# A seven-quarter form of the fifth product from the third row group on, and another order of work in the first two groups

## The chip, the cores and the metric

The kernel runs on one core of one Trainium2 chip. The metric is device microseconds (us) of that core for one execution; a kernel's time is the median of several. Every other time here comes from one profiled execution of the kernel before, in which the program's own span is 1494.3 us. Engines are named as in the profile: PE (matrix multiply), DVE (vector), ACT (scalar), POOL (GpSimd), SP (the engine from whose queue nearly all DMAs go out).

## The reference

```python
B, S, D = 8, 2048, 2048          # x: (8, 2048, 2048) float32, w: (2048, 2048) float32
cs = np.cumsum(x, axis=1)
diff = cs - concatenate([zeros, cs[:, :-1, :]], axis=1)
return np.matmul(diff, w).astype(np.float32)
```

The difference of a running sum with itself one step earlier is x again, so what is computed is one matrix product: x as 16384 x 2048, times w, 2048 x 2048.

## The kernel before

**Rows.** The 16384 rows are 128 row tiles of 128 rows. The first four (tiles 0 to 3) are multiplied plainly in bf16 while w arrives. The other 124 go in 31 groups of four: `group_plain(4)` is the first group, `group(8)`, `group(12)`, `group(16)` are the second, third and fourth, and so on to `group(124)`. In a group, g and h = g + 2 are the upper row blocks of two pairs and g + 1 and h + 1 the lower ones.

**The outer scheme.** Each pair of row tiles and the whole of w are cut into 2 x 2 blocks, and seven products with sums of blocks take the place of eight: A11·B11, A12·B21, S1·T1, S2·T2, S3·T3, S4·B22 and A22·T4. S1 to S4 are sums of quarters of x (f16, made on DVE by `total`, 128x1024 each), T1 to T4 differences of blocks of w (made on DVE by `less`, once, in the first group, 8 pieces each). One product for one pair is 16 matmuls of 128x128 by 128x512 (`steps`, L514), so a group of two pairs has 14 x 16 = 224.

**The inner scheme.** A product for the two pairs together (32 matmuls) can itself be cut once more into seven quarter products of four matmuls (`quarter`, L533): 28. It needs quarter sums of the block of w on the right: Q1, Q2, Q3, Q4, held by a class `Inner` (in_2 for B21, in_3 for B22, in_4 for T4, in_5 for T1). `first()` makes Q1 and Q2 (8 pieces of 128x512), `fourth()` makes Q4 (4 pieces), `third()` makes Q3 in the place of t12 (4 pieces). It also needs sums of quarters of the left side, made by `one()` and `two()` of `sums_in`, four small sums on DVE. From the second group on A12·B21, S4·B22 and A22·T4 have this form: 212 matmuls. Where `five` is true, which is from the fourth group on (`g > PLAIN + 8`), S1·T1 has it too: 208.

**Banks and results.** The eight banks of PSUM are the pairs X and Y and the single banks q, e, v, w (Z and V are pairs in the first group). A result block c (128x512 f32) is begun by `keep` (ACT, L541: copy out of PSUM with a scale) and added to by `add` (DVE, L544: one PSUM bank times a scale plus c); `put` stores it from SP's queue. There are seven such c buffers in a list `free`: `pair()` takes two from its front, `put` appends at its end. In the first group C11h lies in the tile `inner` instead, in pieces 16 to 19, which only later hold quarter sums, so it doesn't go into the list (`del free[-2:]`). One set of four pieces, `flow` (`passed`), holds Q4 for three of the `Inner`s in turn: what is not at hand lies in a DRAM buffer and is stored by `keep_flow(i)` and fetched by `bring_flow(i)`.

**Tiles of x.** Each tile is loaded in two halves (`load`, SP), weighed (`weigh`, ACT, L112: sum of magnitudes of each row), given a scale (`scale_of`: two small instructions on DVE, L129 and L131, and one on POOL, L132, for the unit u), narrowed to f16 (`narrow`, ACT, L143) and transposed by DMA in two halves (`turn`, SP, L156) into one of four places, where it overwrites the tile of the group before.

**Order.** The order on each engine is written out by hand. Every instruction goes through `after(engine, ...)`, which pins it behind the last one of that engine:

```python
    def after(engine, ask):
        if engine in last:
            with tc.issue_after(last[engine].ins):
                said = ask()
```

So an engine works strictly in the order of the calls in `group_plain` and `group`, and an instruction that waits holds up all that stand behind it on its engine.

Of the kernel before, what the change touches and what calls it, by code (L numbers as in the profile page):

```python
# [10 lines left out]
def kernel(  # L11
# [6 lines left out]
    nc = tc.nc  # L18
# [11 lines left out]
    f32 = mybir.dt.float32  # L30
    ADD = mybir.AluOpType.add
# [44 lines left out]
# [4 lines that stand above are left out]
        else:  # L80
            said = ask()
        last[engine] = said[-1] if isinstance(said, tuple) else said
        return said
# [37 lines left out]
    def scale_of(t):  # L121
        if t < END:
            m2 = sums_of.pop(t)
            m = small.tile([P, 1], f32, name="m1")
            s = scales[t] = small.tile([P, 1], f32, name="s")
            u = unit[t] = units.tile([P, 1], f32, name="u")
            after(
                "dve",
                lambda: nc.vector.tensor_scalar(m, m2[:, :1], m2[:, 1:], TINY, ADD, MAX),  # L129
            )  # L130
            after("dve", lambda: nc.vector.reciprocal(s, m))  # L131
            after("pool", lambda: nc.gpsimd.tensor_scalar(u, m, uw, None, MUL))  # L132
# [4 lines left out]
    def narrow(t, sides=range(2)):  # L137
        if t < END:
            s = scales[t]
            for i in sides:  # L140
                after(
                    "act",
                    lambda: nc.scalar.activation(  # L143
                        narrowed(t)[:, ds(i * NH, NH)], where[t][i], COPY, scale=s
                    ),
                )
# [316 lines left out]
    def pair():  # L463
        return [one_c() for _ in range(2)]
# [5 lines left out]
    class Inner:  # L470
# [14 lines left out]
                self.Q4 = [spare.pop() for _ in range(4)]  # L485
            less(self.Q4, self.t21, self.Q2)

        def third(self):
            less(self.t12, self.t22, self.t12)

    passed = [flow[:, k, :] for k in range(4)]

# [3 lines left out]
    def bring_flow(i):  # L496
        after("sp", lambda: nc.sync.dma_start(flow, spill[i - 1]))

    def less(dst, p, q):
        for k in range(len(dst)):  # L500
            after("dve", lambda: nc.vector.tensor_tensor(dst[k], p[k], q[k], SUB))  # L501

    def total(dst, p, q, op):
        after("dve", lambda: nc.vector.tensor_tensor(dst.all, p.all, q.all, op))  # L504
# [21 lines left out]
    def product(to, a, b, first):  # L526
        for some in steps(to, a, b, first, 4):
            some()
# [21 lines left out]
    def adds(c, p, u):  # L550
        for n in range(2):
            add(c[n], p[n], u)
# [7 lines left out]
    def puts(c, t, h):  # L560
        for n in range(2):
            put(c[n], t, 2 * h + n)
# [26 lines left out]
    def group_plain(g, X, Y, Z, V):  # L589
        h = g + 2  # L590
        ug, uh, vg = unit[g], unit[h], unit[g + 1]
        A11g, A12g = parts(g)
        A11h, A12h = parts(h)
        A21g, A22g = parts(g + 1)
        A21h, A22h = parts(h + 1)
        S1g, S1h = S1
        S2g, S2h, S3g, S3h, S4g, S4h = A11g, A11h, A21g, A21h, A12g, A12h
        load(g + 4, 0)
        load(g + 4, 1)
        product(X, A11g, B11, True)  # L600
        for k in range(3):
            block(B22, 1, 1, k, "act")
        C11g = pair()
        keeps(C11g, X, ug)
        for k in range(3, KH):
            block(B22, 1, 1, k, "act" if k < 6 else "dve")
        product(V, A12g, B21, True)
        product(Y, A11h, B11, True)
        adds(C11g, V, ug)
        puts(C11g, g, 0)  # L610
        total(S1g, A21g, A22g, ADD)
        total(S3g, A11g, A21g, SUB)
        total(S2g, S1g, A11g, SUB)
        less(T2[:4], B22[:4], T1[:4])
        product(Z, A12h, B21, True)
        weigh(h + 1)
        C11h = [inner[:, ds(j, 2), :].rearrange("p a n -> p (a n)").bitcast(f32) for j in (16, 18)]
        keeps(C11h, Y, uh)
        scale_of(h + 1)
        narrow(h + 1)  # L620
        turn(h + 1)
        load(h + 4, 0)
        less(T2[4:], B22[4:], T1[4:])
        vh = unit[h + 1]
        product(V, S1g, T1, True)
        C22 = pair()
        keeps(C22, V, vg)
        total(S4g, A12g, S2g, SUB)
        product(X, S2g, T2, False)
        C12g = pair()  # L630
        keeps(C12g, X, ug)
        less(T3, B22, B12)
        product(V, S4g, B22, False)
        weigh(g + 4)
        scale_of(g + 4)
        narrow(g + 4)
        load(h + 4, 1)
        turn(g + 4)
        load(g + 5, 0)
        load(g + 5, 1)  # L640
        product(X, S3g, T3, False)
        total(S1h, A21h, A22h, ADD)
        total(S3h, A11h, A21h, SUB)
        total(S2h, S1h, A11h, SUB)
        adds(C11h, Z, uh)
        puts(C11h, h, 0)
        del free[-2:]
        adds(C12g, V, ug)
        puts(C12g, g, 1)
        product(Y, S2h, T2, False)  # L650
        C12h = pair()
        keeps(C12h, Y, uh)
        adds(C22, X, vg)
        puts(C22, g + 1, 1)
        total(S4h, A12h, S2h, SUB)
        product(Z, S1h, T1, True)
        weigh(h + 4)
        less(T4, B21, T2)
        scale_of(h + 4)
        C22 = pair()  # L660
        keeps(C22, Z, vh)
        narrow(h + 4)
        weigh(g + 5)
        product(Y, S3h, T3, False)
        in_2.first()
        in_2.fourth()
        load(h + 5, 0)
        load(h + 5, 1)
        scale_of(g + 5)
        adds(C22, Y, vh)  # L670
        puts(C22, h + 1, 1)
        product(Z, S4h, B22, False)
        in_2.third()
        adds(C12h, Z, uh)
        puts(C12h, h, 1)
        narrow(g + 5)
        turn(h + 4)
        product(X, A22g, T4, False)
        C21 = pair()
        keeps(C21, X, vg)  # L680
        puts(C21, g + 1, 0)
        turn(g + 5)
        load(g + 8, 0)
        load(g + 8, 1)
        product(Y, A22h, T4, False)
        weigh(h + 5)
        less(in_3.Q1, in_3.t12, in_3.t11)
        scale_of(h + 5)
        narrow(h + 5)
        less(in_3.Q2, in_3.t22, in_3.Q1)  # L690
        turn(h + 5)
        C21 = pair()
        keeps(C21, Y, vh)
        puts(C21, h + 1, 0)


    def group(g, X, Y, q, e, v, w):
        h = g + 2
        five = g > PLAIN + 8
        A11g, A12g = parts(g)  # L700
        A11h, A12h = parts(h)
        A21g, A22g = parts(g + 1)
# [51 lines left out]
        a11, a12, a22, s1, s2, s3, s4 = A2  # L754
        Q = in_2
        quarter(q, a11, Q.t11, True)
        add(C11g[0], q, ug)
        quarter(e, s1, Q.Q1, True)
        add(C11h[1], e, uh)
        if g == PLAIN + 4:  # L760
            total(S1g, A21g, A22g, ADD)
            total(S3g, A11g, A21g, SUB)
            total(S2g, S1g, A11g, SUB)
        quarter(v, a12, Q.t21, True)
        add(C11g[0], v, ug)
# [3 lines left out]
        quarter(e, s4, Q.t22, False)  # L769
        add(C11g[1], e, ug)  # L770
        put(C11g[1], g, 1)
        if g > PLAIN + 4:
            total(S1h, A21h, A22h, ADD)
            total(S3h, A11h, A21h, SUB)
        scale_of(next_g)
        narrow(next_g)
        if g > PLAIN + 4:
            total(S2h, S1h, A11h, SUB)
        go(P6g, 2)
        quarter(q, s3, Q.Q3, False)  # L780
        add(C11h[1], q, uh)
        put(C11h[1], h, 1)
        if g == PLAIN + 4:
            total(S1h, A21h, A22h, ADD)
            total(S3h, A11h, A21h, SUB)
            total(S2h, S1h, A11h, SUB)
        weigh(next_h)
        load(next_k, 1)
        total(S4g, A12g, S2g, SUB)
        go(P6g, 2)  # L790
        C12g = pair()
        keeps(C12g, X, ug)
        turn(next_g, [0])
        quarter(q, a22, Q.Q4, False)
        add(C11h[0], q, uh)
# [5 lines left out]
        if five:  # L801
            one()
            two()
        scale_of(next_h)
        narrow(next_h)
        load(next_l, 1)
        one, two, A3 = sums_in(
            S4g, S4h, (S2h.half(0), S2h.half(1), S4h.half(0), passing[2])
        )
# [6 lines left out]
        if five:  # L816
# [17 lines left out]
            quarter(w, b11, R.t11, True)  # L834
            add(C12g[0], w, ug)
            quarter(v, b12, passed, False)
            bring_flow(1)
            add(C12g[0], v, ug)
            put(C12g[0], g, 2)
            turn(next_g, [1])  # L840
# [53 lines left out]
            put(C12h[1], h, 3)  # L894
            scale_of(next_l)
        else:
            if g == PLAIN + 4:
                in_3.third()
            one()
            two()  # L900
            weigh(next_k)
            seven(A3, in_3, C12g, C12h, P7g)
            turn(next_g, [1])
            turn(next_h, [0])
            scale_of(next_k)
            narrow(next_k)
            Q = in_4 if g == PLAIN + 4 else in_5
            Q.first()
            product((v, w), S1g, T1, True)
            C22g = pair()  # L910
            keeps(C22g, (v, w), vg)
            adds(C12g, (v, w), ug)
            puts(C12g, g, 1)
            load(next_l, 0)
            Q.fourth()
            keep_flow(2 if g == PLAIN + 4 else 1)
            product((q, e), S1h, T1, True)
            C22h = pair()
            keeps(C22h, (q, e), vh)
            adds(C12h, (q, e), uh)  # L920
            puts(C12h, h, 1)
            if g > PLAIN + 4:
                bring_flow(2)
            go(P7g, 2)
            one4()
            two4()
            turn(next_k, [0])
            adds(C22g, X, vg)
            puts(C22g, g + 1, 1)
            if g == PLAIN + 4:  # L930
                in_4.third()
            go(P7h, 4)
            adds(C22h, Y, vh)
            puts(C22h, h + 1, 1)
# [35 lines left out]
        if next_g < END:  # L970
            less(passed, in_2.t21, in_2.Q2)
        turn(next_l, [1])
        if g == PLAIN + 8:
            in_5.third()

    banks = [bank(i) for i in range(8)]
# [35 lines left out]
```

## Time and profile before

| | |
|---|---|
| median of the runs | 1492.88 us (1492.49 to 1496.3, 3 runs) |
| the profiled execution, its own time | 1496.11 us |
| its span | 1494.3 us |
| PE busy | 1473.4 us, 99% |
| DVE busy | 1283.9 us, 86% |
| ACT busy | 913.6 us, 61% |
| POOL busy | 69.4 us, 5% |
| DMA queue of SP | 379.41 MB, 92.6% of 16 engines |
| granted clock of PE | 0.999 |

How to read it: a line of a group of instructions has the line of the code, the engine, the operation, result and operands with their shapes, the count, and the mean length of one. A matmul is counted with 379 ns, but matmuls overlap, and in a full row one starts every 0.216 us. An idle time in square brackets stands in front of the instruction that it precedes, with what ended it. The groups begin at 76.05 (the first), 127.47, 177.44, 223.69 and 270.94 us.

### The profile page before, as it was taken

The numbers are of one execution on the slowest core, as the hardware profiler recorded it, in microseconds if no ns is written. First come the engines' busy times: TensorE is split into PE (matmuls) and PEld (weight loads), VectorE is DVE, ScalarE is ACT, GpSimd is POOL, SyncE is SP. The second block draws the span as 40 slices with busy tenths as digits, with TensorE's granted clock in tenths as the row PEclk, the third lists the DMA queues.
The fourth block names the chain that finished last, engine by engine and source line by source line (L and its number), as shares of the span: only waits on it lengthen the run. The fifth ranks groups of instructions, "written<-read, shape, count | busy, mean of one in ns | idle before, by whom it ended". The sixth has DMA issues, their size and how long they took to land.

```text
span 1494.3 us, 21105 instructions
## 1 busy us (share of the span) xinstructions
PE 1473.4 (99%) x6793; PEld 663.4 (44%) x6799; DVE 1283.9 (86%) x2419; ACT 913.6 (61%) x1301; POOL 69.4 (5%) x136
## 2 busy tenths in 40 slices
PE   8999999999999999999999999999999999999998
PEld 3444444444444444444444444444444444444443
DVE  7997878888888888888888888888888888888887
ACT  5876565655666656666656656556657556656542
POOL 0110000000000000000000000000000000000000
PEclk9999999999999999999999999999999999999999
DMA  9999979999999999999999998999899999899973
GB/s 362 352 233 254 244 224 255 263 271 249 259 258 241 260 276 250 255 251 251 265 269 242 266 248 255 261 272 248 257 239 261 268 257 262 252 238 265 273 204 130
DMA packets 386255, 382.59 MB, mean 256 GB/s; under 512 B 275744, under 2 KB 275744, under 8 KB 386016
## 3 DMA queue, kind: packets, MB, share of 16 engines
q1 hardware_dynamic: 385584, 379.41, 92.6%
q0 software_dynamic: 560, 1.84, 0.3%
q8 instruction: 53, 0.87, 0.2%
q14 instruction: 58, 0.48, 0.1%
HBM read 180.88 MB, written 135.27 MB: 212 GB/s over the span
## 4 chain that ended last, share of the span: by engine, by line
PE 88%; DMA 5%; DVE 3%; ACT 2%; issue 1%; SPq 1%; DVEq 0%; ACTq 0%
PE b L533 45%; PE b L514 41%; DVE c L544 2%; PE b L250 2%; DMA W<-in_w_dram 2%; DMA F<-in_x_dram 2%; DMA x<-F 1%; DVE W L501 1%; ACT waste L112 0%; DMA W<-in_x_dram 0%; DMA out_dram<-wb 0%; ACT F L143 0%; SPq L156 0%; DVE x L504 0%; ACT wb L234 0%
## 5 line engine op out<-in xcount | busy, mean ns | idle before, releaser
L544 DVE SCALAR_TENSOR_TENSOR c<-b,u,c 128x512 f32<-128x512 f32 x1046 | 743.2, 746 | 161.6 <-PE b L533 91.5
L514 PE MATMUL b<-W,x 128*128 128x512 f16 x3072 | 717.4, 379 | 4.3 <-ACT c L541 3.5
L541 ACT ACTIVATE c<-b,u 128x512 f32<-128x512 f32 x494 | 315.9, 681 | 334.5 <-PE b L533 164.0
L514 PEld LDWEIGHTS <-x 128*128 128x128 f16 x3072 | 300.3, 98 | 369.1 <-issue 6.3
L143 ACT ACTIVATE F<-F,s 128x1024 f16<-128x1024 f32 x246 | 282.2, 1147 | 111.2 <-DVE s L131 107.2
L533 PE MATMUL b<-W,inner 128*128 128x512 f16 x1392 | 338.3, 379 | 0.0
L112 ACT ACTIVATE waste<-F 128x1024 uint8<-128x1024 f32 x246 | 259.6, 1055 | 107.5 <-DMA F<-in_x_dram 103.7
L533 PEld LDWEIGHTS <-inner 128*128 128x128 f16 x1744 | 170.6, 98 | 207.1 <-issue 1.6
L533 PEld LDWEIGHTS <-x 128*128 128x128 f16 x1560 | 152.4, 98 | 192.3 <-issue 12.2
L533 PE MATMUL b<-W,x 128*128 128x512 f16 x968 | 234.3, 379 | 1.7 <-DVE c L544 0.3
L504 DVE TENSOR_TENSOR x<-x,x 128x1024 f16<-128x1024 f16 (+1 forms) x214 | 120.5, 574 | 6.2 <-PE b L514 1.1
L132 POOL TENSOR_SCALAR u<-m,uw 128x1 f32<-128x1 f32 x124 | 64.4, 525 | 1311.3 <-DVE m L129 1303.3
L533 PE MATMUL b<-flow,x 128*128 128x512 f16 x352 | 90.3, 379 | 0.7 <-DVE c L544 0.7
L504 DVE TENSOR_TENSOR inner<-x,x 128x1024 f16<-128x1024 f16 (+1 forms) x122 | 67.5, 553 | 1.2 <-DMA x<-F 1.1
L533 PE MATMUL b<-inner 128*128 128x512 f16 x240 | 61.6, 379 | 1.1 <-DVE c L544 1.1
L250 PE MATMUL b<-wb,xP 128*128 128x512 bf16 x234 | 57.0, 393 | 5.4 <-ACT wb L234 3.8
L533 PE MATMUL b<-inner,x 128*128 128x512 f16 x240 | 61.6, 379 | 0.0
L112 ACT ACTIVATION_READ_ACCUMULATOR waste<-F 128x1 f32 x246 | 46.6, 190 | 0.0
L504 DVE TENSOR_TENSOR x<-inner,x 128x1024 f16<-128x1024 f16 x62 | 42.4, 684 | 3.2
L504 DVE TENSOR_TENSOR inner<-inner 128x512 f16<-128x512 f16 x112 | 42.4, 420 | 1.0
L501 DVE TENSOR_TENSOR flow<-W,inner 128x512 f16<-128x512 f16 x120 | 42.6, 416 | 0.0
L234 ACT CAST wb<-W 128x1024 bf16<-128x1024 f32 x32 | 32.2, 1059 | 15.6 <-DMA W<-in_w_dram 12.3
(56 smaller groups left out, 420.0 us busy)
## 6 DMA issues: line engine op xcount, KB each, us to landing
out_dram<-c SPq DMA_DIRECT2D x494, 256.0 KB, 4.1
F<-in_x_dram SPq DMA_DIRECT2D x246, 512.0 KB, 5.2
flow<-spill SPq DMA_DIRECT2D x57, 512.0 KB, 4.8
W<-in_w_dram SPq DMA_DIRECT2D x32, 512.0 KB, 10.0
W<-in_x_dram SPq DMA_DIRECT2D x16, 256.0 KB, 7.2
x<-F SPq DMA_TRANSPOSE x246, 4.0
out_dram<-o POOLq DMA_DIRECT2D x5, 256.0 KB, 4.1
out_dram<-o SPq DMA_DIRECT2D x5, 256.0 KB, 3.6
```

Of the source, the lines that this page charges most:

```text
L112: lambda: nc.scalar.activation(waste, where[t][i], ABS, scale=1.0 / ROW, accum_out=sums_of[t][:, i : i + 1],),
L132: after("pool", lambda: nc.gpsimd.tensor_scalar(u, m, uw, None, MUL))
L143: lambda: nc.scalar.activation(narrowed(t)[:, ds(i * NH, NH)], where[t][i], COPY, scale=s),
L234: after("act", lambda: nc.scalar.copy(b, wt))
L250: lambda: nc.tensor.matmul(ps[r][n], xP[:, r, ko, :], wb[h, ko][:, ds(n * NB, NB)], start=(ko == 0), stop=(ko == KO - 1),),
L501: after("dve", lambda: nc.vector.tensor_tensor(dst[k], p[k], q[k], SUB))
L504: after("dve", lambda: nc.vector.tensor_tensor(dst.all, p.all, q.all, op))
L514: said = nc.tensor.matmul(to[n], a[k], b[k][:, n, :], start=(first and k == 0), stop=(k == KH - 1), skip_group_check=True,)
L533: said = nc.tensor.matmul(to, a[k], b[k], start=(first and k == 0), stop=(k == 3), skip_group_check=True)
L541: after("act", lambda: nc.scalar.activation(c, p, COPY, scale=u))
L544: after("dve", lambda: nc.vector.scalar_tensor_tensor(c, p, u, c, MUL, ADD))
```

## The change

It has three parts.

In `group_plain`, T2's pieces are made in four portions instead of two. The first C22 gets a place in `inner` (pieces 20 to 23) and leaves the list `free`. Its keep, and the keep of the last C21, go ahead of the narrowings that stood before them on ACT. T4 is made in two halves with a scale between them. The weighing of tile h + 5 moves ahead of the keep of the first C21. On SP the turns of h + 4 and g + 5 are taken apart and moved, and the loads of g + 8 go behind the turns of h + 5.

In `group(8)`, the sums S1g and S3g go in front of the first adds, and S1h, S3h, S2h in front of the third quarter; scale and narrowing of the next g go behind it, the weighing of the next h behind a keep, and its scale and narrowing, with a load, behind `one()` and `two()`. in_5.first is new there, in_4.third goes to POOL, in_4.fourth with its store is later, in_5.third is new at the end.

`five` is true from `group(12)` on, one group sooner; there in_5.fourth and a store of flow stand where later groups fetch it.

```diff
-        def third(self):
-            less(self.t12, self.t22, self.t12)
+        def third(self, engine="dve"):
+            less(self.t12, self.t22, self.t12, engine)
...
-    def less(dst, p, q):
+    def less(dst, p, q, engine="dve"):
+        on = {"dve": nc.vector, "pool": nc.gpsimd}[engine]
         for k in range(len(dst)):
-            after("dve", lambda: nc.vector.tensor_tensor(dst[k], p[k], q[k], SUB))
+            after(engine, lambda: on.tensor_tensor(dst[k], p[k], q[k], SUB))
...
         product(Y, A11h, B11, True)
+        less(T2[:1], B22[:1], T1[:1])
         adds(C11g, V, ug)
         puts(C11g, g, 0)
+        less(T2[1:2], B22[1:2], T1[1:2])
         total(S1g, A21g, A22g, ADD)
         total(S3g, A11g, A21g, SUB)
         total(S2g, S1g, A11g, SUB)
-        less(T2[:4], B22[:4], T1[:4])
+        less(T2[2:6], B22[2:6], T1[2:6])
...
         keeps(C11h, Y, uh)
         scale_of(h + 1)
+        less(T2[6:], B22[6:], T1[6:])
+        vh = unit[h + 1]
+        product(V, S1g, T1, True)
+        keeps(C22g, V, vg)
         narrow(h + 1)
         turn(h + 1)
         load(h + 4, 0)
-        less(T2[4:], B22[4:], T1[4:])
-        vh = unit[h + 1]
-        product(V, S1g, T1, True)
-        C22 = pair()
-        keeps(C22, V, vg)
...
-        adds(C22, X, vg)
-        puts(C22, g + 1, 1)
+        adds(C22g, X, vg)
+        puts(C22g, g + 1, 1)
+        del free[-2:]
...
-        less(T4, B21, T2)
+        less(T4[:4], B21[:4], T2[:4])
         scale_of(h + 4)
-        C22 = pair()
-        keeps(C22, Z, vh)
+        less(T4[4:], B21[4:], T2[4:])
+        C22h = pair()
+        keeps(C22h, Z, vh)
...
         load(h + 5, 1)
+        turn(h + 4, [0])
         scale_of(g + 5)
...
         narrow(g + 5)
-        turn(h + 4)
+        weigh(h + 5)
+        turn(h + 4, [1])
+        turn(g + 5, [0])
         product(X, A22g, T4, False)
         C21 = pair()
         keeps(C21, X, vg)
         puts(C21, g + 1, 0)
-        turn(g + 5)
-        load(g + 8, 0)
-        load(g + 8, 1)
+        turn(g + 5, [1])
         product(Y, A22h, T4, False)
-        weigh(h + 5)
         less(in_3.Q1, in_3.t12, in_3.t11)
         scale_of(h + 5)
+        C21 = pair()
+        keeps(C21, Y, vh)
         narrow(h + 5)
         less(in_3.Q2, in_3.t22, in_3.Q1)
         turn(h + 5)
-        C21 = pair()
-        keeps(C21, Y, vh)
+        load(g + 8, 0)
+        load(g + 8, 1)
         puts(C21, h + 1, 0)
...
-        five = g > PLAIN + 8
+        five = g > PLAIN + 4
...
         quarter(q, a11, Q.t11, True)
+        if g == PLAIN + 4:
+            total(S1g, A21g, A22g, ADD)
         add(C11g[0], q, ug)
+        if g == PLAIN + 4:
+            total(S3g, A11g, A21g, SUB)
         quarter(e, s1, Q.Q1, True)
         add(C11h[1], e, uh)
         if g == PLAIN + 4:
-            total(S1g, A21g, A22g, ADD)
-            total(S3g, A11g, A21g, SUB)
             total(S2g, S1g, A11g, SUB)
...
         put(C11g[1], g, 1)
+        total(S1h, A21h, A22h, ADD)
+        total(S3h, A11h, A21h, SUB)
+        if g == PLAIN + 4:
+            total(S2h, S1h, A11h, SUB)
         if g > PLAIN + 4:
-            total(S1h, A21h, A22h, ADD)
-            total(S3h, A11h, A21h, SUB)
-        scale_of(next_g)
-        narrow(next_g)
-        if g > PLAIN + 4:
+            scale_of(next_g)
+            narrow(next_g)
             total(S2h, S1h, A11h, SUB)
...
         put(C11h[1], h, 1)
         if g == PLAIN + 4:
-            total(S1h, A21h, A22h, ADD)
-            total(S3h, A11h, A21h, SUB)
-            total(S2h, S1h, A11h, SUB)
-        weigh(next_h)
+            scale_of(next_g)
+            narrow(next_g)
+        else:
+            weigh(next_h)
...
         keeps(C12g, X, ug)
+        if g == PLAIN + 4:
+            weigh(next_h)
...
-        scale_of(next_h)
-        narrow(next_h)
-        load(next_l, 1)
+        if g > PLAIN + 4:
+            scale_of(next_h)
+            narrow(next_h)
+            load(next_l, 1)
...
-            bring_flow(1)
+            if g == PLAIN + 8:
+                in_5.fourth()
+                keep_flow(1)
+            else:
+                bring_flow(1)
...
         else:
-            if g == PLAIN + 4:
-                in_3.third()
+            in_3.third()
             one()
             two()
+            scale_of(next_h)
+            narrow(next_h)
+            load(next_l, 1)
             weigh(next_k)
             seven(A3, in_3, C12g, C12h, P7g)
             turn(next_g, [1])
             turn(next_h, [0])
+            load(next_l, 0)
             scale_of(next_k)
             narrow(next_k)
-            Q = in_4 if g == PLAIN + 4 else in_5
-            Q.first()
+            in_5.first()
             product((v, w), S1g, T1, True)
...
-            load(next_l, 0)
-            Q.fourth()
-            keep_flow(2 if g == PLAIN + 4 else 1)
+            in_4.first()
+            in_4.third("pool")
             product((q, e), S1h, T1, True)
...
-            if g > PLAIN + 4:
-                bring_flow(2)
             go(P7g, 2)
             one4()
             two4()
             turn(next_k, [0])
             adds(C22g, X, vg)
             puts(C22g, g + 1, 1)
-            if g == PLAIN + 4:
-                in_4.third()
+            in_4.fourth()
+            keep_flow(2)
             go(P7h, 4)
...
-        if g == PLAIN + 8:
+        if g == PLAIN + 4:
             in_5.third()
```

More of the change, by code (lines that the diff above doesn't have):

```diff
@@ L613, in group_plain @@
         total(S2g, S1g, A11g, SUB)
-        less(T2[:4], B22[:4], T1[:4])
+        less(T2[2:6], B22[2:6], T1[2:6])
         product(Z, A12h, B21, True)
         weigh(h + 1)
-        C11h = [inner[:, ds(j, 2), :].rearrange("p a n -> p (a n)").bitcast(f32) for j in (16, 18)]
+        C11h, C22g = (
+            [
+                inner[:, ds(j, 2), :].rearrange("p a n -> p (a n)").bitcast(f32)
+                for j in (i, i + 2)
+            ]
+            for i in (16, 20)
+        )
         keeps(C11h, Y, uh)
         scale_of(h + 1)
+        less(T2[6:], B22[6:], T1[6:])
+        vh = unit[h + 1]
+        product(V, S1g, T1, True)
+        keeps(C22g, V, vg)
         narrow(h + 1)
@@ L668, in group_plain @@
         load(h + 5, 1)
+        turn(h + 4, [0])
         scale_of(g + 5)
-        adds(C22, Y, vh)
-        puts(C22, h + 1, 1)
+        adds(C22h, Y, vh)
+        puts(C22h, h + 1, 1)
         product(Z, S4h, B22, False)
```

## The prediction

> **What bounds the kernel now.** I read the page's shares first (PE busy 99% of a span of 1494.3 us, DVE 86%, ACT 61%, POOL 5%), then the timeline of PE, which shows where a group of four row tiles begins, then the busy time between those beginnings. Columns of the first view: stretch and its length in us, busy us of each engine (instructions), granted clock, DMA share, GB/s.
>
> ```profile
> core 0: us, PE busy (x) PEld busy (x) DVE busy (x) ACT busy (x) POOL busy (x), PEclk, DMA share, GB/s
> 76.05:127.47 51.42, 49.46 (x225) 21.91 (x224) 45.10 (x89) 39.01 (x54) 4.63 (x5) 1.00 0.84 240
> 127.47:177.44 49.97, 47.26 (x213) 20.55 (x212) 38.31 (x85) 31.07 (x46) 3.05 (x5) 1.00 0.96 240
> 177.44:223.69 46.25, 46.20 (x214) 20.69 (x213) 36.12 (x73) 27.77 (x42) 2.46 (x4) 1.00 0.86 238
> 223.69:270.94 47.25, 45.37 (x210) 20.34 (x208) 40.28 (x80) 27.57 (x41) 1.92 (x4) 1.00 1.00 265
> 270.94:316.04 45.10, 45.05 (x210) 20.34 (x208) 39.30 (x76) 28.23 (x41) 1.92 (x4) 1.00 0.96 259
> 316.04:1443.54 1127.50, 1126.33 (x5202) 508.58 (x5201) 982.70 (x1876) 693.85 (x1002) 47.94 (x100) 1.00 0.95 256
> ```
>
> The last row is 25 groups of 45.10. The code orders 224 matmuls in the first group, 212 in the second and third, 208 after. A steady row of 64 (76.05 to 89.86) gives 0.2158 each, so 208 take 44.89 and a steady group loses 0.21. PE at full clock is the bound. Without stalls the first four would take 48.34, 45.75, 45.75 and 44.89; they lose 3.08, 4.22, 0.50 and 2.36. Only these groups' code changes; from the fourth on it is the same. If the first three took 48.34, 46.25 (the third's old length) and 45.10, and the fourth 45.10, the gain would be 194.89 - 184.79 = 10.1, the most there is. The timeline of PE (start, length, what, count, idle before it and its releaser) says where it lies:
>
> ```profile
> 93.31 4.40 PE L514 MATMUL b<-W,x 128*128 128x512 f16 x16
> 98.15 0.38 PE L514 MATMUL b<-W,x 128*128 128x512 f16 x1 [0.44 <-ACT c L541]
> 117.33 13.76 PE L514 MATMUL b<-W,x 128*128 128x512 f16 x63 [1.18 <-ACT c L541]
> 131.48 0.38 PE L514 MATMUL b<-W,x 128*128 128x512 f16 x1 [0.40 <-ACT c L541]
> 140.18 1.90 PE L514 MATMUL b<-W,x 128*128 128x512 f16 x8 [0.40 <-DVE x L504]
> 145.84 3.63 PE L514 MATMUL b<-W,x 128*128 128x512 f16 x16 [0.31 <-DVE x L504]
> 150.33 0.38 PE L514 MATMUL b<-W,x 128*128 128x512 f16 x1 [0.86 <-ACT c L541]
> 234.45 1.02 PE L533 MATMUL b<-inner 128*128 128x512 f16 x4 [1.11 <-DVE c L544]
> 241.38 1.02 PE L533 MATMUL b<-flow,x 128*128 128x512 f16 x4 [0.73 <-DVE c L544]
> ```
>
> Idle time understates a stall, as a last matmul counts 0.38: I take starts less counts by 0.2158.
>
> **First group.** (a) 112.32 to 117.33 holds 17 matmuls (3.67): 1.34 lost, since a keep on ACT waited 3.55 for a C buffer's store. One pair now lives in inner, so two buffers more are free at that point: gain 1.34. (b) 93.31 to 98.73 holds 17: 1.75 lost, to the last halves of T2 (on DVE at 94.59 to 97.07, after 2.12 idle in wait for a scale) and to the keep of V behind a narrowing. Now six T2 pieces precede the scale, and the keep runs at 95.3 to 96.6, so S4g·B22 can begin near 96.8. What is late next is S2h. ACT runs from 94.06 two pairs of keeps (1.25 each), the narrowing (2.33), a pair of keeps, and the weighing of tile 8 (2.37), to 102.5; the scale on DVE waits for it, and S1h, S3h, S2h (0.7 each, before at 102.72) still end near 105.0. PE wants S2h at 96.8 + 32 x 0.2158 = 103.7 and got to it before at 105.4: gain 0.4. The two early T2 pieces (1.24) put S1g at 88.2 to 88.9, before PE's 89.86. The turn of tile 7 goes out 1.3 later and lands (3.2 median in this stretch) just before S1h wants it. Together +1.8: the second group begins at 125.7.
>
> **Second group, to its fifth product.** (c) 131.48 and the start after it lose 0.55 + 0.36 = 0.91, the keep of C21h behind a narrowing (128.53 to 130.86). Now it comes first, at 125.9 to 127.1, for a need at 129.1: +0.9. The weighing of tile 11 (2.4) moves ahead of the keep of C21: ACT 121.95 to 124.3, keep to 125.55, PE's need 125.7. That is just hidden; a load landing 1 late would cost 1. The loads of tile 12 move behind the turns of tile 11 on SP, each turn 1.3 of issue: they go out near 132.1 (133.29 before), its weighing ends near 140.7, and its scale has its turn on DVE only at 141.6. (d) S1g and S3g move into DVE's idle 2.40 before the first add: of 0.57 lost at 140.18, 0.2 stays if the second turn of tile 9 (out at 128.2, 5.0 median in this stretch) lands at 133.2: +0.4. (e) 145.84 loses 0.48 for S2h; the totals now come before the add that frees bank q, which ends near 141.55 for a need of 141.2: 0.45 back, so 0. (f) 150.33 and its next lose 1.04 + 0.36 behind the weighing of tile 14, now behind the keep: +1.4. The scale of tile 14 goes behind one() and two(), near 148, ahead of the first add, whose bank is done at 147.7. So S1g·T1 starts near 154.6, 159.11 before.
>
> **Second group's end.** DVE gets in_5.first, 8 pieces x 0.355 = 2.83, in front of the adds; in_4.third (1.42) leaves it, in_5.third (1.42) comes after the last quarter. Before, that stretch idled 0.31 + 0.67 + 1.08 on DVE. The adds behind run some 1.5 later against PE; the quarter s3 waits for its bank 0.5 instead of 0.21: -0.3. GpSimd's four subtractions have no row. From below, DVE's 0.355 each; from above, ACT's 0.68 for 512 columns and POOL's longest small instruction, 1.36: 2.04. I take POOL's shortest, 0.28, and DVE's one-column-a-cycle pass, 0.75: 1.03 each, 4.1 in all. They start when in_4.first ends (near 163 on this scale) and are wanted near 171.5: hidden up to 2.1 each. The next unit waits behind them on POOL and is wanted a group later. But the two engines meet:
>
> ```profile
> 114.53 0.83 POOL L132 TENSOR_SCALAR u<-m,uw 128x1 f32<-128x1 f32 x1 [11.04 <-DVE m L129]
> 114.55 1.41 DVE L501 TENSOR_TENSOR inner<-W 128x512 f16<-128x512 f16 x4
> 122.13 0.28 POOL L132 TENSOR_SCALAR u<-m,uw 128x1 f32<-128x1 f32 x1 [6.78 <-DVE m L129]
> 122.15 1.39 DVE L544 SCALAR_TENSOR_TENSOR c<-b,u,c 128x512 f32<-128x512 f32 x2
> ```
>
> The same POOL instruction takes 0.28 beside adds and 0.83 beside SBUF subtractions. So they hold each other up; that a long POOL instruction holds DVE, no row shows. From below 0, from above 4.1 less 0.6 of slack in front of the quarter into X[0]: 3.5. The first falls beside adds; three meet one4, two4 and in_4.fourth, half of each: 1.5 - 0.6, I take -1.0. [...]
>
> **Third and fourth group.** Four matmuls fewer (32 to 28), 0.86, and the other form's own waits, 0.29: +1.15. in_5.fourth (1.42) stands where a 512 KB load stood; DVE then adds in one row from 254.19 to 259.73 on the old fourth group's clock, and the quarter into bank e at 260.37 needs one that ended at 259.0: -0.2 (from 0 to -1.4). For the fourth group, the chain of waits shows why it loses 2.15 over 45.10:
>
> ```profile
> 222.34 7.70 DMA x<-F
> 230.06 0.44 DVE inner L504
> ```
>
> A turn goes out 1.35 before the group ends, lands 7.70 later, and DVE starts the sums 6.37 after the beginning, against 3.30 in the group after (274.24). A third group in the new form ends as the later ones do: +2.15. But the second now has its flow stored late, between the stores of C22, and I put its turn at 1.6 before its end: the same fault one group sooner, from 0 to -2.15, taken as -1.2, since no load waits there for a store (2.5 on SP before).
>
> **Sum:** 1.8 + 0.9 + 0.4 + 0 + 1.4 - 0.3 - 1.0 + 1.15 - 0.2 - 1.2 + 2.15 = 5.1, all against the profiled span: 1494.3 becomes 1489.2. That execution took 1496.11 outside, while the runs have a median of 1492.88 (1492.49 to 1496.3); the difference I carry over: 1487.8.
>
> **Rivals.**
> 1. No lock and the turns in time: 5.1 + 1.0 + 1.2 = 7.3, 1485.6; all stalls gone, 1482.8. For it: the third group began without a wait after a tail of the same length. Against: new DVE work in the second group. Chance 0.15.
> 2. The lock whole, 3.5 for 1.0: 1490.3. For it, POOL's own 0.83; against, the first subtraction has adds beside it. 0.15.
> 3. DMA takes the early gain back (share 0.96 in the second group): turns of tiles 9 and 12's loads late, so (d) and (f) fail, 1.8, and the fourth group's 2.15 comes whole in the third, 0.95 more: 1490.5. For it, weighings there waited 1.58, 1.30 and 2.08 for loads. 0.10.
> 4. Slower: the lateness is carried on. Each steady group waits 0.21 at its last quarter for an add; DMA is at 0.95. If the tails settle later, every one of 28 groups pays: it decides from 5.1 / 28 = 0.18 each, and at twice that, 0.36, the time is 1487.8 + 10.1 = 1497.9. Against: the old fourth group was 2.15 late and the next took 45.10 at once. 0.12.
>
> The forecast has 0.48, with its own range 1486 to 1490 (the lock and the turns at their ends, not together). A measurement tells 0.3%, 4.5 us, from no change: 1488.4 and 1497.4 bound it. Of the forecast some 0.35 lies below 1488.4; with rival 1, faster 0.50; rival 4 slower, 0.12; the rest 0.38. The range, 1483.5 to 1494, leaves out most of rival 4 and the end of rival 1.
>
> **What would show it.** (a), (b): no idle for a C buffer near 115 and S2h·T2 starting near 105.0. (c), (f): no PE idle released by ACT's L541. Second group near 48.6, third 46.5, fourth 45.1. POOL: four instructions near 1 us, DVE subtractions longer beside them. Wrong if a steady group is not 45.10, or if the last quarter of the second group waits for POOL.

## The result and the profile after

The changed kernel takes 1489.86 us (median of 6 runs, 1488.87 to 1490.62), the one before 1494.82 (6 runs, 1492.49 to 1497.16): ratio 0.9966, 95% interval 0.9954 to 0.9979, or 4.96 us less. The forecast was 5.1 us less, or 1487.8 us, reckoned from the 1492.88 that the kernel before had in 3 runs; in 6 runs its median is 1.94 higher. The profiled execution of the changed kernel has a span of 1488.0.

The busy time between the group starts of the changed kernel (length, busy us of PE, weight loads, DVE, ACT, POOL, then clock, DMA share, GB/s):

```profile
core 0: us, PE busy (x) PEld busy (x) DVE busy (x) ACT busy (x) POOL busy (x), PEclk, DMA share, GB/s
75.15:124.84 49.69, 48.60 (x225) 21.79 (x224) 46.37 (x95) 39.43 (x56) 5.99 (x6) 1.00 0.94 260
124.84:174.36 49.52, 46.57 (x213) 20.64 (x212) 41.85 (x84) 30.54 (x43) 7.25 (x8) 1.00 0.82 225
174.36:219.54 45.18, 45.13 (x210) 20.32 (x208) 41.59 (x84) 26.80 (x40) 1.92 (x4) 1.00 0.95 269
219.54:264.64 45.10, 45.05 (x209) 20.34 (x208) 39.40 (x76) 28.91 (x42) 1.92 (x4) 1.00 0.95 261
...
309.74:1437.24 1127.50, 1126.33 (x5201) 508.60 (x5200) 982.63 (x1876) 694.36 (x1002) 47.95 (x100) 1.00 0.95 256
```

The first four groups take 189.49 instead of 194.89: 5.40 less. Another 0.90 of the span's difference lies in front of them (start at 75.15 instead of 76.05), where no code changed; over all profiles below that start lies between 74.71 and 76.78. The steady groups take 45.10 as before (1127.50 for 25). The third and fourth already run at that pace; the second has gained only 0.45. PE's timeline has the waits that are left:

```profile
92.42 10.60 PE L515 MATMUL b<-W,x 128*128 128x512 f16 x48
104.11 3.63 PE L515 MATMUL b<-W,x 128*128 128x512 f16 x16 [1.09 <-DVE x L505]
...
111.03 20.88 PE L515 MATMUL b<-W,x 128*128 128x512 f16 x96
...
152.79 7.07 PE L515 MATMUL b<-W,inner 128*128 128x512 f16 x32
...
165.67 1.02 PE L534 MATMUL b<-W,x 128*128 128x512 f16 x4 [0.63 <-DVE c L545]
168.52 1.02 PE L534 MATMUL b<-W,x 128*128 128x512 f16 x4 [1.83 <-DVE c L545]
...
173.49 1.04 PE L534 MATMUL b<-W,x 128*128 128x512 f16 x4 [0.49 <-DVE c L545]
```

All idle times that ACT ended (98.15, 117.33, 131.48, 150.33 before) are gone, and 96 matmuls run through from the first group into the second. Left in the first group is the wait for S2h; new are three waits for DVE's adds in the last 9 us of the second. DVE and POOL in front of them:

```profile
158.36 3.34 DVE L502 TENSOR_TENSOR W<-W 128x512 f16<-128x512 f16 x4
158.92 5.09 POOL L502 TENSOR_TENSOR W<-W,W 128x512 f16<-128x512 f16 x4 [4.13 <-DVE W L502]
161.62 3.33 DVE L502 TENSOR_TENSOR W<-W,W 128x512 f16<-128x512 f16 x4
164.88 1.40 DVE L545 SCALAR_TENSOR_TENSOR c<-b,u,c 128x512 f32<-128x512 f32 x2
```

Four subtractions took DVE 1.41 elsewhere; beside GpSimd's in_4.third the eight of in_4.first take from 158.36 to 164.88. From S1g·T1 (152.79) to the end the second group needs 21.57, against 18.33 before: 3.24 lost. The start of S1g·T1 before, from which the 18.33 are counted to 177.44:

```profile
159.11 7.07 PE L514 MATMUL b<-W,inner 128*128 128x512 f16 x32
```

### The profile page after: what moved, and what is told of

It reads as the page before. It is cut to its first block, busy times and chain, and to the rows that moved or that the text cites. A ratio compares the mean times of both kernels' runs of the same rounds, so it can differ in the third digit from the quotient of the medians.

```text
span 1488.0 us, 21123 instructions
## 1 busy us (share of the span) xinstructions
PE 1470.6 (99%) x6789; PEld 663.2 (45%) x6795; DVE 1293.4 (87%) x2430; ACT 913.8 (61%) x1301; POOL 74.5 (5%) x140
## 4 chain that ended last, share of the span: by engine, by line
PE 91%; DMA 3%; DVE 3%; ACT 2%; issue 1%; SPq 0%; DVEq 0%; ACTq 0%
PE b L534 47%; PE b L515 43%; DVE c L545 2%; PE b L250 2%; DMA W<-in_w_dram 2%; DMA F<-in_x_dram 1%; DVE W L502 0%; DMA W<-in_x_dram 0%; DMA out_dram<-wb 0%; ACT F L143 0%; ACT waste L112 0%; ACT wb L234 0%; ACT W L361 0%; ACT o L270 0%; ACT c L542 0%
## 5 line engine op out<-in xcount | busy, mean ns | idle before, releaser
L534 PE MATMUL b<-W,inner 128*128 128x512 f16 x1416 | 344.1, 379 | 0.0
L237 DVE TENSOR_REDUCE wmax<-W 128x1 f32<-128x1024 f32 x32 | 38.9, 1219 | 3.4 <-DMA W<-in_w_dram 2.0
```

The source lines that it names most:

```text
L237: lambda: nc.vector.tensor_reduce(wmax[:, i : i + 1], wt, AX.X, MAX, apply_absolute_value=True),
L534: said = nc.tensor.matmul(to, a[k], b[k], start=(first and k == 0), stop=(k == 3), skip_group_check=True)
```

## The experiments

All lengths are group lengths from one profiled execution each, read as above; a start inside a merged row is counted on at 0.2158 a matmul. `first_new`, `bring_pool` and `bring_act` change the kernel before, the others the changed one.

| run | first | second | third | fourth | sum | sum without the first |
|---|---|---|---|---|---|---|
| before | 51.42 | 49.97 | 46.25 | 47.25 | 194.89 | 143.47 |
| after | 49.69 | 49.52 | 45.18 | 45.10 | 189.49 | 139.80 |
| third_dve | 48.48 | 47.02 | 45.67 | 45.10 | 186.27 | 137.79 |
| third_dve_timed | 48.34 | 47.02 | 45.82 | 45.10 | 186.28 | 137.94 |
| third_late | 48.80 | 47.02 | 46.02 | 45.10 | 186.94 | 138.14 |
| third_half | 49.95 | 48.28 | 45.10 | 45.10 | 188.43 | 138.48 |
| split | 49.53 | 48.37 | 45.29 | 45.10 | 188.29 | 138.76 |
| idle_pool | 48.34 | 52.86 | 45.10 | 45.10 | 191.40 | 143.06 |
| no_five | 48.34 | 46.29 | 46.25 | 47.26 | 188.14 | 139.80 |
| first_new | 48.91 | 47.30 | 46.24 | 47.23 | 189.68 | 140.77 |
| first_old | 51.03 | 54.50 | 45.19 | 45.10 | 195.82 | 144.79 |
| c22_pair | 49.91 | 51.14 | 45.10 | 45.10 | 191.25 | 141.34 |
| bring_pool | 51.64 | 50.25 | 51.73 | 46.16 | 199.78 | 148.14 |
| bring_act | 51.59 | 50.55 | 46.81 | 45.10 | 194.05 | 142.46 |

### Does GpSimd hold DVE up, and how much for one instruction?

**third_dve:** the four subtractions back on DVE, in the same place.

```diff
-            in_4.third("pool")
+            in_4.third()
```

> in_4.third goes back to DVE at the place where it now goes to GpSimd. After the change DVE's eight in_4.first subtractions beside GpSimd's four took 6.6 us (158.36 to 164.95) instead of 2.83, and the second group's end lost 3.24 over its old 18.33. Theory (the two engines lock each other out): DVE needs 2.83 + 1.42 = 4.25 there, 2.4 less, and the second group falls from 49.52 to about 47.2, the third stays at 45.2 or grows by up to 1 as its turn goes out earlier against DMA. Rival (it is the added DVE work in front of the adds that makes the end late): moving 1.42 more to DVE makes the second group 50.5 to 51.

The timeline of PE's S1g·T1 and of DVE:

```profile
151.26 7.07 PE L515 MATMUL b<-W,inner 128*128 128x512 f16 x32
...
156.84 1.42 DVE L502 TENSOR_TENSOR W<-W 128x512 f16<-128x512 f16 x4
158.17 2.77 DVE L502 TENSOR_TENSOR W<-W,W 128x512 f16<-128x512 f16 x8
160.86 1.40 DVE L545 SCALAR_TENSOR_TENSOR c<-b,u,c 128x512 f32<-128x512 f32 x2
```

Twelve subtractions from 156.84 to 160.86, 0.335 each. From S1g·T1 to the end the group takes 19.07, which loses 0.74 instead of 3.24. The second group falls to 47.02; the third grows by 0.5, where DVE waits 0.89 for a turned tile before S1h. More work on DVE and less time: the added work was not the cause.

**third_half:** two pieces each.

```diff
-            in_4.third("pool")
+            less(in_4.t12[:2], in_4.t22[:2], in_4.t12[:2], "pool")
+            less(in_4.t12[2:], in_4.t22[2:], in_4.t12[2:])
```

> Two of the four in_4.third pieces stay on GpSimd, two go to DVE. Theory (lock, one GpSimd instruction holds DVE for about its own length): DVE's time from the first piece of in_4.first to the first add behind is 2.83 + 0.71 + 2 x 0.96 = 5.5 us, between 6.6 and 4.25, and the second group is near 48.4. Rival (added DVE work): near 50. Rival (a start-up cost of GpSimd's first instruction of this kind): nearly all of the 3.8 stays, group at 49.5 or more.

DVE's stretch up to the first add is 5.27 for ten subtractions, 3.35 of its own at 0.335. What GpSimd adds is 1.92 for two instructions, and 6.52 - 8 x 0.335 = 3.84 for four: 0.96 for each, with no start-up. The second group is at 48.28.

**idle_pool:** GpSimd subtracts quarters of B21 into flow, which nobody needs; third on DVE.

```diff
+            if g == PLAIN + 4:
+                less(passed, in_2.t11, in_2.t21, "pool")
             in_5.first()
...
-            in_4.third("pool")
+            in_4.third()
```

> in_4.third is on DVE as in the first of these runs, and in the second group GpSimd makes four subtractions nobody needs: quarters of B21 into flow, tiles that DVE's in_5.first beside it (blocks of T1 into other places) neither reads nor writes. Theory (lock of the two engines, whatever the tiles): in_5.first takes 2.83 + 3 to 4 us, each DVE subtraction beside GpSimd near 0.8 instead of 0.355. Rival (the two were slow because both read t12 and t22 of T4): in_5.first stays at 2.83.

DVE and POOL:

```profile
152.53 2.37 DVE L502 TENSOR_TENSOR W<-W 128x512 f16<-128x512 f16 x4
153.30 5.20 POOL L502 TENSOR_TENSOR flow<-W,W 128x512 f16<-128x512 f16 x4
154.82 3.96 DVE L502 TENSOR_TENSOR W<-W,W 128x512 f16<-128x512 f16 x3
...
159.04 1.40 DVE L545 SCALAR_TENSOR_TENSOR c<-b,u,c 128x512 f32<-128x512 f32 x2
```

The eight of in_5.first go from 152.53 to 159.04: 6.51, 3.83 more than their own 2.68, with no tile in common with GpSimd's. So it is the engines that meet, not the tiles. Their rows alternate: in the changed kernel GpSimd's start at 158.92, 160.09, 161.38 and 162.68, and DVE's long subtractions behind them at 159.03, 160.33, 161.62 and 162.92, one every 1.30, which is 0.335 + 0.96. So a GpSimd instruction here costs DVE 0.96. The second group as a whole, 52.86, is longer than these 3.83 explain, for a reason told at the end.

**split:** Q1 of in_4 in front of the adds into C12h, Q2 behind them.

```diff
-            in_4.first()
+            less(in_4.Q1, in_4.t12, in_4.t11)
             in_4.third("pool")
...
             puts(C12h, h, 1)
+            less(in_4.Q2, in_4.t22, in_4.Q1)
```

> GpSimd keeps in_4.third, but DVE makes only Q1 of in_4 (four pieces) before the adds into C12h, and Q2 behind them, so GpSimd runs mostly beside adds, which read one operand from PSUM, and beside DVE's idle time. Theory (lock only against two SBUF operands): Q1 takes up to 1.42 + 2, the adds stay at 1.40 a pair, the end of the second group loses 1 to 1.5 instead of 3.24, group near 47.5. Rival (GpSimd slows every DVE instruction): adds longer than 1.40 a pair, group 49 or more.

```profile
158.04 3.34 DVE L502 TENSOR_TENSOR W<-W 128x512 f16<-128x512 f16 x4
161.30 1.40 DVE L545 SCALAR_TENSOR_TENSOR c<-b,u,c 128x512 f32<-128x512 f32 x2
162.62 2.17 DVE L502 TENSOR_TENSOR W<-W,W 128x512 f16<-128x512 f16 x4
```

GpSimd runs from 158.59 to 163.50, across all three rows. Subtractions on both sides are longer (Q1 starts 3.26 before the adds, 1.34 of its own; Q2 2.10), the adds, with one operand from PSUM, keep their 1.40. That is the theory; but only a quarter of GpSimd's work fell beside the adds, and the group came to 48.37, not 47.5.

### Where do the other gains come from?

**first_new:** the kernel before with the first group's function of the change, and nothing else of it: its edit is the part of the change that lies in `group_plain`.

> The kernel before with only the first group's function of the change. Theory: first group 49.7, second 49.97 - 0.9 = 49.0, third 46.25 and fourth 47.25 as before; sum 192.2, 2.7 under before. Rival (loads of tiles 12 and the others come later against PE and the second group gives it back): second group 50.5 or more, sum near 194.9.

The expectation is beaten: the second group gains 2.67, not 0.9, with its own code unchanged. 0.92 of it is the expected one, the keep of C21h that now stands in front of a narrowing. Of the rest, 1.39 is the stall at 150.33 and 0.32 a part of that at 156.38. For the stall at 150.33, SP's queue says why. Before:

```profile
134.37 5.92 SPq L156 DMA_TRANSPOSE x<-F  x2
141.48 1.75 SPq L100 DMA_DIRECT2D F<-in_x_dram  x3
```

and with the first group's new order:

```profile
127.37 4.24 SPq L156 DMA_TRANSPOSE x<-F  x3
135.11 2.43 SPq L100 DMA_DIRECT2D F<-in_x_dram  x3
...
143.14 4.49 PE L514 MATMUL b<-W,x 128*128 128x512 f16 x20 [0.31 <-DVE x L504]
```

Before, the two turns of tile 11 held SP for 5.92, and the loads of tiles 14 and 13 behind them went out 14.0 after the group's start (127.47). Now three turns go through in 4.24, and the loads go out 9.4 after it (125.69). The weighing of tile 14 doesn't wait for DMA any more (2.08 before), so the keep that stands behind it and cost PE 1.39 at 150.33 is in time: the 20 matmuls from 143.14 run through. This is read from the queue; no run changes SP's order alone. The waits before 140.18 and 145.84, (d) and (e) of the prediction, stay (0.57 and 0.47).

**first_old:** the reverse, the changed kernel with the old first group.

> The changed kernel with the first group's function as it was before: order of T2 and T4, C22 in the ring of C buffers, keeps behind narrowings, turns and loads in the old order. Theory (the first group's stalls were local and are gone for good): the first group is 51.4 again, the second 49.5 + 0.9 = 50.4 or a little more, the third 45.2, the fourth 45.1. Rival (the lateness is absorbed by slack later): second group 48 to 49.

The second group takes 54.50, 4.1 more than expected. DVE and PE:

```profile
142.02 0.69 DVE L505 TENSOR_TENSOR inner<-x,x 128x1024 f16<-128x1024 f16 x1 [2.27 <-DMA x<-F]
...
144.88 1.50 PE L534 MATMUL b<-flow,x 128*128 128x512 f16 x4 [2.25 <-DVE c L545]
```

S1h now stands ahead of the add that frees bank q. With the old first group, tile 11's turns land late, DVE waits 2.27 at S1h, and the add and PE wait behind it: PE loses 2.42 there. The other 1.7 is a slow stretch of PE right behind that wait (told at the end). The stall at 150.33 is gone here too, as the keep now stands in front of the weighing. So with the old first group, the 2.43 that the new order saves at (d), (e) and (f) is lost again at S1h.

**no_five:** the fifth product's form and its sums as before; the new order of the first group and of the second up to its fifth product stays.

```diff
-        five = g > PLAIN + 4
+        five = g > PLAIN + 8
...
-            in_5.first()
+            Q = in_4 if g == PLAIN + 4 else in_5
+            Q.first()
...
-            in_4.first()
-            in_4.third("pool")
+            load(next_l, 0)
+            Q.fourth()
+            keep_flow(2 if g == PLAIN + 4 else 1)
```

> The changed kernel with the fifth product as before: plain in the third group, in_4's sums in the second and in_5's in the third, all on DVE; the new order of the first group and of the second up to its fifth product stays. Theory (new order and earlier form are separate gains): second group 46.5 to 47, third 46.25, fourth 47.25. Rival (the new order of the second group brings nothing once the first is mended): second group 47.3, as with the first group's new function alone.

46.29, 46.25 and 47.26, as the theory has it. So the second group's order is worth another 47.30 - 46.29 = 1.01: (d) and (e). Without the first group, whose length varies (below), the sum is 139.80, the very sum of the whole change: the earlier form of the fifth product, as written, brings nothing. With the subtractions on DVE it brings 139.80 - 137.94 = 1.86 (third_dve_timed; 2.01 by third_dve, 1.66 by third_late below).

**c22_pair:** the first C22 from the ring of C buffers again.

```diff
-        C11h, C22g = (
...
-        )
+        C11h = [inner[:, ds(j, 2), :].rearrange("p a n -> p (a n)").bitcast(f32) for j in (16, 18)]
...
+        C22g = pair()
         keeps(C22g, V, vg)
...
-        del free[-2:]
```

> The changed kernel, but the first C22 is taken from the ring of C buffers again instead of inner. Theory: ACT's keep of the second C22 waits for a store of C12g again (3.55 before), PE loses up to 1.34 near 111 to 117, first group 49.7 + 1.0 to 1.3. Rival (the earlier order has made the store early enough): first group 49.7 as now.

The 17 matmuls from 112.27 end at 116.47: 4.20 for 3.67, so 0.53 lost and not 1.34. With 1.03 lost at S2h that makes the first group 49.91. ACT's keep still waits 2.75, but it starts earlier. The result lies between theory and rival: the order around it had taken most of the 1.34. Its second group is longer for another reason, told at the end.

**bring_pool:** the fetch of flow in the old third group from GpSimd's queue instead of SP's.

```diff
-                bring_flow(2)
+                after("pool", lambda: nc.gpsimd.dma_start(flow, spill[1]))
```

> The kernel before, but in its third group the fetch of flow that waits on SP for the store of flow goes out from GpSimd's queue, so that nothing waits behind it. Theory (the old fourth group loses 2.15 because the turn of tile 18 goes out late behind that wait): the turn goes out 2 to 2.5 earlier against the group's end, the fourth group is 45.1 to 45.6. Rival (the 512 KB of traffic itself delays the turn's landing): still 46.5 to 47.3.

This is inconclusive: the fetch landed 7.17 after its start at 218.09, PE waited 3.89 for it, and the third and fourth group (51.73 and 46.16) can't be read for the question.

**bring_act:** the same from ACT's queue (`nc.scalar`).

> [...] Theory (SP's wait for the store makes the turn of tile 18 late, and that the fourth group's 2.15): the turn goes out 2 or more earlier against the group's end, fourth group 45.1 to 46. Rival (the traffic): 46.5 to 47.3. ACT stands still until the store has landed, so the weighing of tile 19 comes 1 to 2 later, which may cost the fourth group up to 1 by itself.

```profile
217.24 0.38 ACTq L923 DMA_DIRECT2D flow<-spill  x1
...
220.50 1.69 SPq L156 DMA_TRANSPOSE x<-F  x1
...
228.06 0.41 DVE L504 TENSOR_TENSOR inner<-x 128x512 f16<-128x512 f16 x1
```

The turn goes out 3.35 before the group's end (223.85) instead of 1.35, DVE starts the sums 4.2 after it instead of 6.37, and the fourth group takes 45.10. The traffic is the same; SP's wait for the store was the cause of the 2.15. The third group pays 0.56, 0.48 of it in wait for the fetch.

### A version that is faster than the kernel before and perhaps than the change

**third_dve_timed** is the kernel of third_dve once more; **third_late** has the four subtractions on DVE behind in_4.fourth:

```diff
-            in_4.third("pool")
...
             in_4.fourth()
             keep_flow(2)
+            in_4.third()
```

> The changed kernel with in_4.third on DVE in the same place, now timed. One look gave groups of 48.5, 47.0, 45.7 and 45.1 (sum 186.3 against 194.9 before and 189.5 after the change), so 8 us under before and 3 under the change: ratio 0.9945 if the start is the same. If the single look was a lucky start, 0.996 as for the change.

> in_4.third on DVE, but behind in_4.fourth instead of in front of the adds into C12h. The 0.3 that PE lost in front of the quarter into X[0] goes; the 0.65 at the last quarter stays or grows by up to 1, as C22h's adds are no earlier. Same as the one in front within 0.5 us; rival (late subtractions keep the last quarter waiting): 1 to 1.5 slower than that.

1487.65 us (5 runs, ratio to before 0.9951, 0.9938 to 0.9963) and 1486.79 (5 runs, 0.9945, 0.9932 to 0.9959), before 1494.72 (9 runs). The two can't be told from each other: the groups from the second on sum to 137.94 and 138.14. Both are 2 to 3 us under the change (1489.86), but their intervals reach into its own and they were not timed side by side with it. That they are faster than the change rests on the group lengths: from the second group on 1.66 to 2.01 less in three profiles.

## Why the prediction was right, point by point

- **First group, +1.8:** measured 1.73 (51.42 to 49.69). The step on what is late next held: S2h·T2 starts 104.11 - 75.15 = 28.96 after the group's start, and the forecast put it at 105.0 - 76.05 = 28.95. That it fits so closely is partly luck: S2h follows the load of tile 7, which was about as late as before (its weighing began 17.27 after the group's start, 16.95 before), and in the other eight profiles with this first group the gain lies between 1.47 and 3.08. The split was off: the C buffer's own share is 0.53 once the rest is in order (c22_pair), not 1.34.
- **Second group up to S1g·T1, +2.7:** measured 3.69 (31.64 to 27.95). (c), (d) and (f) are gone entirely. (e) is gone too, 0.47 that the forecast put at 0: the add that frees q ended at 140.37 for a need at 140.39. The wait at 156.38 fell from 0.46 to 0.14, for which the forecast has no term. For (f) the prediction named only half of the cause: it gave the gain to the keep that now stands in front of the weighing of tile 14, but with the first group's order alone (first_new) the stall is gone as well, as that tile's load is in time. Either is enough.
- **Second group's end, -0.3 and -1.0:** measured -3.24. This is the term that was mis-sized: 0.74 is left with the work on DVE, so 2.50 is GpSimd's, not 1.0. The length taken for one instruction, 1.03, was an estimate from two rows of the kernel before, POOL's shortest (0.28) and the mean of DVE's adds (L544, 0.75). It is near what one adds to DVE's stretch, 0.96 (its own row is 1.21 to 1.33 beside DVE). The meeting was wrong: the subtractions don't wait for the end of in_4.first but for its first piece, start 0.56 behind it, and four of the eight subtractions of in_4.first take 1.37 each, the others 0.41.
- **Third group, +1.15, -0.2, -1.2:** measured +1.07 in all, at 45.18, against a forecast of -0.25. in_5.fourth cost at most 0.08. The 1.2 for a late turn did not come: the turn went out 1.51 before the end (1.6 forecast), but landed 5.71 later and not 7.70, as in the old third group. That is 4.20 after the group's start; DVE was busy with in_5.third until 4.63, and its sums then were early enough.
- **Fourth group, +2.15:** measured 2.15, with the mechanism shown by bring_act.
- **Rivals:** the two engines did hold each other up, which is the lock that the rivals name, 3.84 on DVE and 2.50 on PE (the second rival had 3.5 on PE); its time did not come, since the late turns cost nothing and the stretch in front gained more than forecast. DMA took nothing back (its share in the second group is 0.82, 0.96 before). No lateness was carried on: the steady groups take 45.10. The sum of terms was 5.1, the groups show 5.40, the medians 4.96. That these lie so close is luck: 1.94 too little loss at the second group's end stands against 0.99 in front of it and 1.32 in the third group.

## What to carry to other kernels

Before work is moved to an idle engine, ask what the two cost each other side by side: here four subtractions that cost DVE 1.34 of its own cost it 3.84 from GpSimd. When a stall is seen behind an instruction, look at the queue that fed it a group earlier: with the first group's new order, the 1.39 at 150.33 went without a change at the place of the stall. And price a moved instruction from its first possible start, not from the end of the block it stands behind in the code.

## What the runs showed of the hardware that was not expected

**PE slows after waits near 2 us, not always.** In c22_pair it loses 2.00 in front of 170.66, as the changed kernel does in front of 168.52 (1.99). The changed kernel runs on at full pace; c22_pair does not:

```profile
core 0: us, PE busy (x) PEld busy (x) DVE busy (x) ACT busy (x) POOL busy (x), PEclk, DMA share, GB/s
166.00:171.00 5.00, 2.53 (x12) 0.98 (x11) 4.89 (x11) 0.69 (x1) 0.14 (x1) 0.98 0.50 141
171.00:177.00 6.00, 5.95 (x21) 2.19 (x20) 4.77 (x12) 2.82 (x4) 0.28 (x1) 0.73 0.94 293
170.81:174.22 3.41, 3.41 (x9) 1.18 (x8) 3.38 (x10) 0.08 (x1) 0.08 (x1) 0.50 0.86 282
```

The granted clock is 0.50 for 3.41 us from 170.81 on. It is 0.50 for as long in first_old (from 145.29, behind a loss of 2.42), and for 6.8 us in idle_pool and bring_pool (from 166.96 and 224.07, within waits of about 2 and 3.9). Part of their long second and third groups is that. Why one of two equal waits (2.00 and 1.99) was followed by a slow stretch and the other was not, no run here shows.

**The first group's length follows one load.** Its code is the same in after, third_dve, third_half, split and the like, yet it took 48.34 to 49.95. The second weighing of tile 7 began 15.33 (third_dve_timed), 16.06 (third_dve), 17.27 (after) and 17.53 (third_half) after the group's start, and the group took 48.34, 48.48, 49.69 and 49.95: past about 16 every microsecond of that load is a microsecond of S2h. It may be one source of the spread of the runs of one kernel, but no run shows that, nor why the load lands earlier or later.
